# Loading the small rows ahead of tile 3's norm, and transposing the bias columns at tile 5

## The chip, the cores and the metric

The kernel runs on one core of a Trainium2 chip. A core has five engines that run side by side, each with its own in-order queue: TensorE (PE; its weight loads are listed as PEld), VectorE (DVE), ScalarE (ACT), GpSimd (POOL) and SyncE (SP), which here issues nearly all the transfers. The time is device microseconds of one execution. Lower is better.

## The reference

One layer of a hybrid decoder on 1024 tokens of width 1024, with 16 learned meta tokens in front, in float32. In outline:

```python
h = concatenate([meta, x])                         # 16 + 1024 tokens, 1024 wide
proj = rms_norm(h, norm_mix) @ w_in + b_in         # split into q, k, v, gates of two branches
log_a = log_sigmoid(g_lr @ gla_w_gate + gla_b_gate) / 16
o_gla = head_rms(gla_chunked(q, k, v, log_a)) * silu(g_r)
qk    = silu(causal_dwconv(concat[m_q, m_k], ml_conv_w, ml_conv_b))
o_ml  = head_rms(mlstm_chunked(...)) * sigmoid(m_o)
y = sigmoid(gate_a) * (o_gla @ w_branch_gla) + sigmoid(gate_b) * (o_ml @ w_branch_ml)
h = h + y @ w_out
u = causal_dwconv(rms_norm(h, norm_ffn) @ w_up, ffn_conv_w, ffn_conv_b)
h = h + (silu(gate) * up) @ w_down
out = rms_norm(h, norm_final)[16:]
```

The change touches only the start: the norm of the input tokens, and the biases that the first projections add.

## The kernel before

Matrix products are made from two-part operands: a value is split into a high part (`H`, rounded by ACT) and a low part (`L`, the rest, by DVE), and a product is the sum of three matmuls, HH, HL and LH. So `xH` and `xL` are the normalized input, channels on partitions, and `wH` and `wL` a weight.

**The input.** The tokens come in nine tiles. Tile 0 holds the 16 meta tokens, tiles 1 to 8 hold 128 tokens each; the number is that of the loop (`i`), so "the fourth tile" is tile 3 and "the sixth" is tile 5. `load_x(i)` issues the 512 KB transfer of a tile into `xt`. `norm_x(i)` then makes, for a tile: the sum of squares on ACT (L342, with a read of the accumulator), mean plus epsilon on DVE (L345), the power -1/2 on POOL (L347), scaling in place on DVE (L349; L353 for tile 1), four transposes on PE into each of two `xtp` tiles (L357), and for each of these the high part on ACT (L359) and the low part on DVE (L361). The `xtp` tiles and the tile of the column transpose share three PSUM buffers (tag `s`).

**The small rows.** `small` is a list of 21 small transfers, from a few bytes to 44 KB: ten go to `va`, which gathers biases and per-channel factors as 106 rows of 128; three to `bsm` (gate biases); two to `wg` (the decay gate's weight and bias); three to `vf` (the convolution of the FFN). (Some of the ten are listed by the trace as one row with a count.) `columns()` transposes `va` on PE into `coltp` (L323), copies it to `col` on DVE (L324) and scales four of its columns (L325). `col` holds, among others, the biases of k and q, which every eviction of their products adds.

**The first projections.** Right behind the norm come k and q of head 0, each over four spans of tokens (called thirds below, from the name of the list in the code): 0 to 272, 272 to 528, 528 to 784 and 784 to 1040 for k, and the same with a slightly shorter first span for q. Their matmuls are L159 with `wH_gk`, `wL_gk`, `wH_gq`, `wL_gq`; a span is 24 matmuls, issued in two halves of 12, k and q in turn. Each goes into one of three PSUM banks (tag `pj`), and ACT drives them out with the bias added: L446 for k (`kT`), L448 for q (`qT`). After them come the v projection (`pv`, L197) and sums and differences of the input's parts on DVE (L1033 and after), operands of a later product.

**What sets the order.** A scheduler orders the instructions of each engine by priorities and by when operands come ready by its own estimate; the written order is the base of these priorities. Evictions and the preparation of weights are given a higher priority (`hp`). Transfers are issued by SP in its own order. Each transfer counts on one of eight semaphores in turn, and waits until the one eight places earlier has landed. The raw weights (`wr`) have two buffers, so the first part of the v weights (`wr_gv`) waits until the k weights are split.

Of the kernel before, what the change touches and what calls it, by code (L numbers as in the profile page):

```python
# [25 lines left out]
NC = SEQ // P  # L26
# [19 lines left out]
def hybrid_kernel(ctx, tc, x, meta, norm_mix, w_in, b_in, gla_w_gate, gla_b_gate, gla_norm,  # L46
                  ml_conv_w, ml_conv_b, ml_norm, w_branch_gla, w_branch_ml, w_out, norm_ffn,
                  ffn_w_up, ffn_conv_w, ffn_conv_b, ffn_w_down, norm_final, out):
    nc = tc.nc
# [9 lines left out]
    def hp(n):  # L59

        return tc.high_priority(offset=max(1, min(n, tc.cur_priority - floor[0])))
# [222 lines left out]
    small = []  # L284
# [35 lines left out]
    def columns():  # L320

        tp = ps.tile([P, 512], F32, name="coltp", tag="s", bufs=3)
        nc.tensor.transpose(tp[:, :nrow], va[:nrow, :], ident[:nrow, :nrow])  # L323
        nc.vector.tensor_copy(col, tp[:, :nrow])  # L324
        nc.vector.tensor_scalar(col[:, C_GQ:C_GQ + 4], col[:, C_GQ:C_GQ + 4], QS, None, OP.mult)  # L325
# [3 lines left out]
    def load_x(*tiles):  # L329
        for i in tiles:  # L330
            n = NM if i == 0 else P
            xt = xt_tiles[i]
            nc.sync.dma_start(xt[:n, :D], meta if i == 0 else x[P * (i - 1):P * i, :])
            xts[i] = xt

    def norm_x(i):
        n = NM if i == 0 else P
        c0 = 0 if i == 0 else NM + P * (i - 1)
        xt = xts[i]
        ss = xs.tile([P, 1], F32, name=f"xss{i}", tag="ss1", bufs=3)  # L340
        junk = xs.tile([P, D], F32, name=f"xj{i}", tag="of", bufs=1)
        nc.scalar.activation(junk[:n, :D], xt[:n, :D], AF.Square, accum_out=ss[:n])  # L342
        with hp(40):
            v = xs.tile([P, 1], F32, name=f"xv{i}", tag="xv", bufs=3)
            nc.vector.tensor_scalar(v[:n], ss[:n], 1.0 / D, EPS, OP.mult, OP.add)  # L345
            rs = xs.tile([P, 1], F32, name=f"xr{i}", tag="xr", bufs=3)
            last = nc.gpsimd.tensor_tensor(rs[:n], v[:n], mhalf[:n], OP.pow)  # L347
        if i != 1:
            nc.vector.scalar_tensor_tensor(xt[:n, :D], xt[:n, :D], rs[:n], gmix[:n], OP.mult, OP.mult)  # L349
        for g in range(2):  # L350
            if i == 1:
                h = slice(512 * g, 512 * (g + 1))
                nc.vector.scalar_tensor_tensor(xt[:, h], xt[:, h], rs, gmix[:, h], OP.mult, OP.mult)  # L353
            tp = ps.tile([P, 4, P], F32, name=f"xtp{i}_{g}", tag="s", bufs=3)
            for j in range(4):
                k = 4 * g + j
                nc.tensor.transpose(tp[:, j, :n], xt[:n, k * P:(k + 1) * P], ident[:n, :n])  # L357
            h4 = xH[:, 4 * g:4 * g + 4, c0:c0 + n]
            nc.scalar.activation(h4, tp[:, :, :n], AF.Copy)  # L359
            l4 = xL[:, 4 * g:4 * g + 4, c0:c0 + n]  # L360
            nc.vector.tensor_tensor(l4, tp[:, :, :n], h4.bitcast(F32), OP.subtract)  # L361
        return last
# [11 lines left out]
    load_x(3)  # L374
    U.get(1, 0)
    load_x(4, 5)
    norm_x(3)
    U.get(2, 0)
    load_x(6, 7, 8)
    for dst, ap in small:  # L380
        nc.sync.dma_start(dst, ap)
    for i in range(4, NC + 1):
        if i == NC:
            columns()
        last = norm_x(i)
    for t, c in ((xH, 0), (xL, 32)):
# [920 lines left out]
    i = 0  # L1307
# [843 lines left out]
    i = FIRST  # L2151
# [87 lines left out]
```

## Time and profile before

| what | us |
|---|---|
| three runs | 1880.22, 1873.54, 1877.35; median 1877.35 |
| profiled execution, its own time | 1882.24 |
| its span (first to last instruction) | 1880.5 |
| PE busy in the span | 1844.2 (98%) |
| DVE, ACT, POOL busy | 1298.8, 931.1, 236.5 |
| mean granted clock of TensorE | 0.992 |

The profile is of one execution. A row of the order of time gives start, length, engine, line, operation, "out<-in" by the program's names, shapes and a count; a bracket at its end gives the idle time of the engine ahead of it and what ended that. A row of the stretches gives a stretch, its length, the busy time of PE, PEld, DVE, ACT and POOL with the number of instructions, then the clock that PE was granted (1.00 is full), the mean busy share of the transfer engines, and GB/s. A matmul's listed length is longer than the step to the next one, since they overlap.

### The profile page before, as it was taken

The page shows a single profiled execution, that of the slowest core. Times are in us where ns is not written, and L with a number is a line of the kernel's source. Part 1 is how long each engine was busy: PE and PEld are TensorE (multiplying, and loading weights), DVE is VectorE, ACT ScalarE, POOL GpSimd, SP SyncE. Part 2 cuts the span into 40 slices and gives each one's busy share as a digit, 9 for nine tenths or more (in the row PEclk, how much of TensorE's full clock was granted, in tenths as well). Part 3 has the DMA queues.
Part 4 walks back from the last instruction along what each step waited for, and adds up shares of the span by engine and source line. Part 5 has one row for each costly group of instructions (what it writes and reads, how often), then busy time and mean ns, then how long its engine had stood idle before and what let it go on. Part 6 is the DMA issues. An engine that isn't in the chain of part 4 may idle for free. (4 is left out here: it accounts for less than half of the span.)

```text
span 1880.5 us, 32830 instructions
## 1 busy us (share of the span) xinstructions
PE 1844.2 (98%) x13158; PEld 1759.1 (94%) x13158; DVE 1298.8 (69%) x1960; ACT 931.1 (50%) x1602; POOL 236.5 (13%) x220
## 2 busy tenths in 40 slices
PE   8999999999999999999999999999999999999997
PEld 6999999999999999898999999999999999987886
DVE  7755555567766467676633655888788899877877
ACT  5445444423456677876431235943443443446755
POOL 3200000000032122000000000012222222200000
PEclk9999999999999999999999999999999999999999
DMA  4244434345523233357667987433333545589985
GB/s 142 84 119 123 118 111 122 106 138 155 173 65 113 65 116 113 102 183 261 241 239 255 329 295 261 130 101 108 107 101 113 159 144 165 178 304 338 357 300 216
DMA packets 256338, 322.13 MB, mean 171 GB/s; under 512 B 14643, under 2 KB 197341, under 8 KB 254521
## 3 DMA queue, kind: packets, MB, share of 16 engines
q1 hardware_dynamic: 256089, 319.93, 51.7%
q8 instruction: 103, 1.69, 0.4%
q14 instruction: 50, 0.41, 0.1%
q0 software_dynamic: 96, 0.10, 0.0%
HBM read 231.59 MB, written 88.40 MB: 170 GB/s over the span
## 5 line engine op out<-in xcount | busy, mean ns | idle before, releaser
L1999 DVE TENSOR_TENSOR ringL<-f,ringH 128x1024 fp32r<-128x1024 f32 x76 | 80.0, 1066 | 19.9 <-ACT ringH L1998 19.5
L1998 ACT ACTIVATE ringH<-f 128x1024 fp32r<-128x1024 f32 x76 | 69.1, 928 | 36.5 <-DMA f<-in_ffn_w_down_dram 24.4
L1865 PE MATMUL po<-wH_wo,yH 128*128 128x256 f32 x256 | 73.6, 288 | 0.0
L1865 PE MATMUL po<-wL_wo,yH 128*128 128x256 f32 x256 | 73.4, 287 | 0.0
L1865 PE MATMUL po<-wH_wo,yL 128*128 128x256 f32 x256 | 73.1, 286 | 0.0
L1814 DVE SCALAR_TENSOR_TENSOR cv<-u,fc,cv 128x1024 f32<-128x1024 f32 x44 | 65.0, 1479 | 0.4
L705 POOL TENSOR_TENSOR pk<-pk,kT 128x256 f32<-128x256 f32 (+1 forms) x40 | 49.8, 1267 | 90.1 <-ACT pk L703 78.3
L1742 POOL TENSOR_TENSOR SB<-SA,rg 128x512 f32<-128x512 f32 x20 | 27.7, 1383 | 233.1 <-DVE SA L1738 120.7
L1090 POOL TENSOR_TENSOR gA<-gu2raw,gA 128x512 fp32r<-128x512 f32 x14 | 18.0, 1286 | 287.8 <-ACT gA L1089 287.8
L1724 POOL TENSOR_TENSOR A<-u2raw,A 128x512 fp32r<-128x512 f32 x20 | 42.7, 2137 | 88.4 <-ACT A L1723 88.4
L1723 ACT ACTIVATE HA<-rg 128x1024 fp32r<-128x1024 f32 x16 | 17.0, 1060 | 72.6 <-PE Y L1765 72.6
L1865 PEld LDWEIGHTS po<-wL_wo,yH 128*128 128x128 f32 x256 | 49.9, 195 | 0.0
L1865 PEld LDWEIGHTS po<-wH_wo,yL 128*128 128x128 f32 x256 | 49.8, 195 | 0.0
L1865 PEld LDWEIGHTS po<-wH_wo,yH 128*128 128x128 f32 x256 | 49.8, 194 | 0.0
L2037 ACT ACTIVATE aH<-f 128x768 fp32r<-128x768 f32 (+1 forms) x38 | 35.4, 934 | 27.9 <-PE dV L2062 14.0
L1792 ACT ACTIVATE u2raw<-X 128x258 f32<-128x258 f32 (+1 forms) x44 | 16.4, 374 | 65.6 <-PE X L1765 65.5
L2038 DVE TENSOR_TENSOR aL<-f,aH 128x768 fp32r<-128x768 f32 (+1 forms) x38 | 40.4, 1067 | 11.7 <-ACT aH L2037 11.2
L1147 ACT ACTIVATE goB<-goB,col 128x256 f32<-128x256 f32 x56 | 28.1, 502 | 37.7 <-DVE goB L1142 22.3
L1486 PE MATMUL bm<-omL,wH_bm 128*128 128x342 f32 x144 | 46.0, 320 | 0.0
L1486 PE MATMUL bm<-omH,wH_bm 128*128 128x342 f32 x144 | 46.0, 320 | 0.0
L1486 PE MATMUL bm<-omH,wL_bm 128*128 128x342 f32 x144 | 46.0, 320 | 0.0
L1147 ACT ACTIVATE goA<-goA,col 128x258 f32<-128x258 f32 (+1 forms) x56 | 28.4, 508 | 35.4 <-DVE goA L1143 28.3
(772 smaller groups left out, 7820.3 us busy)
## 6 DMA issues: line engine op xcount, KB each, us to landing
f<-wts SPq DMA_DIRECT2D x38, 512.0 KB
vr<-in_w_in_dram SPq DMA_DIRECT2D x24, 512.0 KB
wsH<-in_ffn_w_down_dram SPq DMA_DIRECT2D x11, 1024.0 KB
wts<-wsL SPq DMA_DIRECT2D x11, 1024.0 KB
rg<-in_ffn_w_up_dram SPq DMA_DIRECT2D x22, 512.0 KB
ru<-in_ffn_w_up_dram SPq DMA_DIRECT2D x22, 512.0 KB
ad<-a SPq DMA_DIRECT2D x44, 256.0 KB
wr_wo<-in_w_out_dram SPq DMA_DIRECT2D x18, 512.0 KB
```

The costliest lines, as they stand in the source:

```text
L705: nc.gpsimd.tensor_tensor(e, e, k, OP.mult)
L1090: nc.gpsimd.tensor_tensor(t[:, 4:8], g_raw, t[:, 0:4].bitcast(F32), OP.subtract)
L1147: nc.scalar.activation(v, v, func, bias=cc(c + i))
L1486: nc.tensor.matmul(pts[i][:, :n], a[:, k, :], b[k][:, t0:t0 + n], start=(k == 0 and j == 0), stop=(k == NK - 1 and j == 2))
L1724: eng.tensor_tensor(l, src, h.bitcast(F32), OP.subtract)
L1742: late.tensor_tensor(sb[:, 0:4], sa[:, 0:4], rg[:, 0:4], OP.subtract)
L1814: nc.vector.scalar_tensor_tensor(y, u[:, j:SEQ + j], fc[:, j, jj:jj + 1], y, OP.mult, OP.add)
L1865: nc.tensor.matmul(pt[:, :DV], a, b[:, k % 4, :], start=(k == 0 and i == 0), stop=(k == NK - 1 and i == len(terms) - 1))
L1998: nc.scalar.activation(h, raw, AF.Copy)
L1999: splits.append(nc.vector.tensor_tensor(l, raw, h.bitcast(F32), OP.subtract))
L2037: nc.scalar.activation(h, a[:, :n], AF.Copy)
L2038: nc.vector.tensor_tensor(l, a[:, :n], h.bitcast(F32), OP.subtract)
```

## The change

```diff
@@ -374,13 +374,13 @@
     load_x(3)
     U.get(1, 0)
     load_x(4, 5)
+    for dst, ap in small:
+        nc.sync.dma_start(dst, ap)
     norm_x(3)
     U.get(2, 0)
     load_x(6, 7, 8)
-    for dst, ap in small:
-        nc.sync.dma_start(dst, ap)
     for i in range(4, NC + 1):
-        if i == NC:
+        if i == 5:
             columns()
         last = norm_x(i)
```

The transfers of the small rows stand behind the loads of tiles 4 and 5, ahead of the first v weights and of tiles 6 to 8. The columns are transposed ahead of tile 5's norm instead of tile 8's. No instruction is added or taken away. On each engine the same instructions stand in another order, up to the end of the v projection.

On SP, behind the first tiles. Before (`xt6` is tile 6):

```order
L333 DMA xt4_96<-in_x_dram 128x1024
L333 DMA xt5_97<-in_x_dram 128x1024
L333 DMA xt6_98<-in_x_dram 128x1024
L333 DMA xt7_99<-in_x_dram 128x1024
L103 DMA wr_gv0_0_221<-in_w_in_dram 128x3x256
L103 DMA wr_gv0_0_221<-in_w_in_dram 128x3x16
L103 DMA wr_gv0_0_221<-in_w_in_dram 128x3x4
L333 DMA xt8_100<-in_x_dram 128x1024
L103 DMA wr_gv0_0_221<-in_w_in_dram 128x3x4
L381 DMA va_104<-in_b_in_dram 8x128 x4
```

With the change, from the last of the small rows on (the first of them, the same `va` row, follows `xt5`):

```order
L378 DMA vf_107<-in_ffn_conv_b_dram 44x128
L103 DMA wr_gv0_0_239<-in_w_in_dram 128x3x256
L333 DMA xt6_98<-in_x_dram 128x1024
L103 DMA wr_gv0_0_239<-in_w_in_dram 128x3x16
L103 DMA wr_gv0_0_239<-in_w_in_dram 128x3x4
L333 DMA xt7_99<-in_x_dram 128x1024
L333 DMA xt8_100<-in_x_dram 128x1024
```

Tiles 6 and 7 went from ahead of the v weights to behind them and behind all small rows.

On ACT, the squares of tiles 6 and 7 (`xj6`, `xj7`). Before:

```order
L342 ACTIVATE xj6_296,xss6_295<-xt6_98 128x1024
L342 ACTIVATE xj7_318,xss7_317<-xt7_99 128x1024
L359 ACTIVATE xH_88<-xtp3_0_207 128x4x128
L359 ACTIVATE xH_88<-xtp3_1_214 128x4x128
L359 ACTIVATE xH_88<-xtp4_0_259 128x4x128
```

And, further on, the first evictions of k and q, before:

```order
L359 ACTIVATE xH_88<-xtp6_1_310 128x4x128
L359 ACTIVATE xH_88<-xtp7_0_325 128x4x128
L359 ACTIVATE xH_88<-xtp7_1_332 128x4x128
L446 ACTIVATE kT0_385<-pj0_0_387,col_109 128x272
L446 ACTIVATE kT0_385<-pj0_272_439,col_109 128x256
L448 ACTIVATE qT0_386<-pj1_0_400,col_109 128x258
```

The same with the change, where both stand together:

```order
L359 ACTIVATE xH_88<-xtp5_0_285 128x4x128
L446 ACTIVATE kT0_385<-pj0_0_387,col_109 128x272
L359 ACTIVATE xH_88<-xtp5_1_292 128x4x128
L448 ACTIVATE qT0_386<-pj1_0_400,col_109 128x258
L342 ACTIVATE xj6_300,xss6_299<-xt6_98 128x1024
L446 ACTIVATE kT0_385<-pj0_272_439,col_109 128x256
L342 ACTIVATE xj7_322,xss7_321<-xt7_99 128x1024
L359 ACTIVATE xH_88<-xtp6_0_307 128x4x128
L359 ACTIVATE xH_88<-xtp6_1_314 128x4x128
L342 ACTIVATE xj8_344,xss8_343<-xt8_100 128x1024
```

The first evictions went from behind tile 7 to among tile 5, and the squares of tiles 6 and 7 from ahead of tile 3's high part to behind the evictions.

On DVE, around the copy of the columns, with the change:

```order
L361 TENSOR_TENSOR xL_89<-xtp4_1_266,xH_88 128x4x128
L324 COPY col_109<-coltp_273 128x106
L325 TENSOR_SCALAR col_109<-col_109 128x4
L361 TENSOR_TENSOR xL_89<-xtp5_0_285,xH_88 128x4x128
L361 TENSOR_TENSOR xL_89<-xtp5_1_292,xH_88 128x4x128
L345 TENSOR_SCALAR xv6_302<-xss6_299 128x1
L349 SCALAR_TENSOR_TENSOR xt6_98<-xt6_98,xr6_304,gmix_112 128x1024
L345 TENSOR_SCALAR xv7_324<-xss7_321 128x1
L349 SCALAR_TENSOR_TENSOR xt7_99<-xt7_99,xr7_326,gmix_112 128x1024
L361 TENSOR_TENSOR xL_89<-xtp6_0_307,xH_88 128x4x128
```

Before, the copy stood behind the low parts of tile 7; now it stands behind those of tile 4, and the scaling of tile 7 stands ahead of tile 6's low parts. On PE the second q span (`pj1_258`) went from behind tile 7's transposes to ahead of tile 6's.

## The prediction

> **What bounds the kernel now.** I read the busy times first, then PE's stretches near the start, then PE's waits and the order of time around them. One row of the page and two rows of the stretches (length; then busy time of PE, PEld, DVE, ACT and POOL; granted clock; DMA share; GB/s):
>
> ```profile
> PE 1844.2 (98%) x13158; PEld 1759.1 (94%) x13158; DVE 1298.8 (69%) x1960; ACT 931.1 (50%) x1602; POOL 236.5 (13%) x220
> ...
> 22.90:52.40 29.50, 27.32 (x215) 26.39 (x214) 26.56 (x36) 14.63 (x26) 16.23 (x30) 0.94 0.14 31
> 52.40:100.00 47.60, 47.60 (x361) 47.05 (x360) 31.97 (x47) 19.83 (x33) 5.03 (x7) 1.00 0.36 107
> ```
>
> PE sets the time. From 52.4 us on it has no idle time at all up to 100 us, so a microsecond that PE gains before 52.4 us goes on to the end unless something later takes it back. In 22.9 to 52.4 us PE is idle for 2.18 us (29.50 less 27.32) and its clock is not full. All that the change moves lies before about 88 us; behind that the order of the work on PE is the same in both kernels. So the question is what PE loses between 16 and 52 us. The order of time there (start, length, engine, line, what, and in brackets the idle time and what ended it):
>
> ```profile
> 32.21 1.17 PE L357 MATMUL xtp<-ident,xt 128*128 128x128 f32 x8 [0.27 <-DVE xt L349]
> 33.32 0.31 PE L323 MATMUL coltp<-ident,va 106*128 106x106 f32 x1
> 33.51 1.29 DVE L361 TENSOR_TENSOR xL<-xtp,xH 128x512 fp32r<-128x512 f32 x2 [0.24 <-ACT xH L359]
> 34.72 0.26 DVE L324 COPY col<-coltp 128x106 f32<-128x106 f32 x1
> 35.01 0.85 ACT L446 ACTIVATE kT<-pj,col 128x272 f32<-128x272 f32 x2 [0.99 <-DVE col L324]
> 35.55 0.39 PE L159 MATMUL pj<-xH,wH_gq 128*128 128x256 f32 x1 [1.92 <-ACT kT L446]
> ```
>
> The transpose of the bias columns (L323) is issued only at 33.32, its copy on DVE stands behind two subtractions of tile 7, the first k eviction on ACT needs that copy, and PE needs a bank of `pj`, of which there are three, all full: 1.92 us idle. It is followed by a second loss:
>
> ```profile
> 36.15:39.60 3.45, 3.45 (x19) 3.45 (x18) 2.27 (x5) 1.68 (x3) 2.92 (x10) 0.51 0.00 0
> ...
> 36.24 0.41 PE L159 MATMUL pj<-xH,wL_gq 128*128 128x256 f32 x1
> 36.67 1.91 PE L357 MATMUL xtp<-ident,xt 128*128 128x128 f32 x8
> 39.65 0.29 PE L159 MATMUL pj<-xL,wH_gq 128*128 128x256 f32 x1
> 40.95 0.28 PE L159 MATMUL pj<-xH,wH_gk 128*128 128x256 f32 x1
> 52.20 0.28 PE L159 MATMUL pj<-xH,wL_gq 128*128 128x256 f32 x1
> ```
>
> For 3.45 us the granted clock is 0.51. From 40.95 to 52.20 there are 96 matmuls, so one takes 11.25/95 = 0.118 us at full clock.
>
> **The price of the lost clock.** Between the matmuls at 36.24 and 39.65 PE issued eight matmuls and the eight transposes of tile 8. What these cost at full clock follows from tile 5:
>
> ```profile
> 27.40 0.28 PE L159 MATMUL pj<-xH,wH_gk 128*128 128x256 f32 x1
> 27.59 1.06 PE L357 MATMUL xtp<-ident,xt 128*128 128x128 f32 x8
> 28.41 0.36 PE L159 MATMUL pj<-xL,wH_gk 128*128 128x256 f32 x1
> 28.61 0.27 PE L159 MATMUL pj<-xH,wL_gk 128*128 128x256 f32 x1
> ```
>
> Two matmul steps and eight transposes took 1.21 us here, so the transposes cost 1.21 - 2 x 0.118 = 0.97 us. Eight matmuls and the transposes are 0.94 + 0.97 = 1.91 us at full clock; they took 3.41, so the half clock cost 1.50 us. Together with the waits, 1.92 + 0.27 + 1.50 = 3.69 us. That is all this change can win in the place it aims at, 0.2% of the time.
>
> **What it removes: the late column copy.** In the new order `coltp` stands among the first third's q matmuls, between the transposes of tiles 4 and 5, and its copy stands on DVE behind tile 4 instead of tile 7. The order of time around tile 4:
>
> ```profile
> 23.47 0.60 PE L357 MATMUL xtp<-ident,xt 128*128 128x128 f32 x4
> 23.49 1.29 DVE L361 TENSOR_TENSOR xL<-xtp,xH 128x512 fp32r<-128x512 f32 x2 [2.87 <-ACT xH L359]
> ```
>
> The first four transposes of tile 4 start at 23.47. From there, nine k matmuls, five q matmuls and the second half of tile 4 put `coltp` at about 26.0, its copy at 27.1 behind tile 4's last subtraction, and the first k eviction at 28.0 to 28.4. PE wants the bank for the second q third after tile 5's transposes and twelve matmuls of the second k third, at 29.5. So this wait goes, with 1.1 us to spare: minus 1.92, and with it, if no other gap comes, minus 1.50. Tile 5's scaling also goes forward, into DVE's idle 2.87 us ahead of 23.5 us, and the 0.27 us at tile 7 is replaced by what follows.
>
> **What it adds: tiles 6 and 7 are normalized late.** Before, their squares ran early; now ACT has tile 6's square behind the first q eviction, and tile 7's square behind the second k eviction (the order shown ahead). From a square to the transposes there is this chain (rows of different tiles, for their lengths and hand-overs):
>
> ```profile
> 25.43 1.05 ACT L342 ACTIVATE xj<-xt 128x1024 f32<-128x1024 f32 x1
> 26.17 1.27 DVE L349 SCALAR_TENSOR_TENSOR xt<-xt,xr,gmix 128x1024 f32<-128x1024 f32 x1
> 26.37 0.19 ACT L342 ACTIVATION_READ_ACCUMULATOR xj<-xt 128x1 f32 x1
> 28.35 0.14 DVE L345 TENSOR_SCALAR xv<-xss 128x1 f32<-128x1 f32 x1
> 28.63 0.55 POOL L347 TENSOR_TENSOR xr<-xv,mhalf 128x1 f32<-128x1 f32 x1 [3.10 <-DVE xv L345]
> ```
>
> The square and its read, 25.43 to 26.56, take 1.13 us; then 0.14 + 0.55 + 1.27 on DVE, POOL and DVE; the hand-over DVE to POOL is 0.14 (28.49 to 28.63), DVE to PE 0.15 (27.44 to 27.59), and I take 0.04 and 0.05 for the other two. Sum: 3.47 us from the start of a square to the transposes.
>
> Tile 6: its square starts behind the first q eviction, at 29.4, so its transposes can start at 32.9. PE gets there at 33.3. No stall.
>
> Tile 7: take the last matmul of the second k third as zero. Its eviction starts at 0.3 and takes 0.45, the square starts at 0.75, and the transposes of tile 7 can start at 4.2. PE in that time has eight q matmuls (1.06 with the step into them), tile 6's transposes (0.97), four q matmuls and two of the next third (0.7, and about 0.1 for restarts): it is there at 2.85. **It waits 1.37 us.** The second half of tile 7 needs a buffer of the transposes, of which there are three; it is tile 6's first one, drained by a DVE subtraction of 0.68 that stands behind tile 7's scaling: 0.25 us more. ACT's square also sits ahead of tile 6's evictions: 0.15 us. Tile 8's scaling comes behind tile 7's subtractions on DVE and is late by about 0.13 us. Together plus 1.90 us. Bounds: zero, if the squares get ahead of what I assumed; 3 us, if each hand-over is a third longer and two of the waits don't overlap.
>
> **What it moves: 21 small transfers ahead of tiles 6 to 8.** SP's rows, and the square of tile 5:
>
> ```profile
> 4.34 4.58 SPq L333 DMA_DIRECT2D xt<-in_x_dram  x4
> 15.94 1.08 ACT L342 ACTIVATE xj<-xt 128x1024 f32<-128x1024 f32 x1
> 16.73 1.44 SPq L103 DMA_DIRECT2D wr_gv<-in_w_in_dram  x3
> 18.22 0.48 SPq L333 DMA_DIRECT2D xt<-in_x_dram  x1
> 19.22 1.76 SPq L381 DMA_DIRECT2D va<-in_b_in_dram  x5
> 22.93 0.32 SPq L381 DMA_DIRECT2D va<-in_ml_conv_w_dram  x1
> 23.29 0.31 SPq L381 DMA_DIRECT2D va<-in_ml_conv_b_dram  x1
> 27.46 0.35 SPq L381 DMA_DIRECT2D vf<-in_ffn_conv_b_dram  x1
> ```
>
> SP stood still from 8.9 to 16.7 us ahead of the value weights, and the small transfers now go into that gap. They don't all fit: from the eighth on, each waits until an earlier transfer on its semaphore has landed, the eighth for tile 5, which was there by 15.94, when its square began. From the eighth's issue to the end of the last one was 4.5 us (23.29 to 27.81), so the value weights and tile 6 come at 20.4 to 21 us instead of 16.7 and 8. A 512 KB tile behind small pieces landed 4.7 us after its issue (18.22 to 22.93, where the next transfer waited for it): tile 6 by 25.7, tiles 7 and 8 by about 27.5. Their squares want them at 29.4, 33.1 and 35.4. So this costs nothing, the cover being 3.7 us for tile 6; without it each microsecond costs one. `va` is wanted at 26 and is complete by 18; `vf` is wanted at 44 and is complete by 23.
>
> **Sum.** 1882.24 (the profiled execution, span 1880.5) - 3.69 + 1.90 = 1880.45, that is 1.8 us less. The median of the three runs is 4.9 us below the profiled execution; set against it, **1875.5 us**.
>
> **The clock, the largest rival.** Whether a gap costs the clock is decided between these (two waits near 2 us and one of 1.2, and the stretch after each):
>
> ```profile
> 796.90 0.33 PE L627 MATMUL ot<-ident,or 128*128 128x128 f32 x1 [1.90 <-ACT or L615]
> 1158.30 0.65 PE L1676 MATMUL htp<-ident,hn 2*128 2x2 f32 x8 [2.22 <-ACT hn L1661]
> 759.91 0.35 PE L741 MATMUL sc<-pk 128*128 128x128 f32 x1 [1.24 <-ACT An L735]
> ...
> 796.90:800.30 3.40, 3.40 (x15) 3.01 (x15) 1.41 (x7) 2.74 (x7) 0.00 (x0) 0.57 0.54 158
> 1159.20:1162.50 3.30, 3.30 (x18) 3.30 (x17) 1.65 (x2) 2.58 (x10) 0.55 (x1) 0.50 0.96 310
> 759.90:763.30 3.40, 3.38 (x25) 3.40 (x26) 1.86 (x2) 3.33 (x9) 0.00 (x0) 1.00 0.00 0
> ```
>
> Gaps of 1.90 and 2.22 us, like the 1.92 above, were followed by some 3.4 us at half clock; a gap of 1.24 was not. The new gap, 1.37 and 0.25 with transposes between and on both sides, lies between them, nearer to the harmless one. [...]
>
> **The rivals.** B: the new gap costs the clock. Then 1.50 us comes back: -3.69 + 1.90 + 1.50 = -0.3, **1877.1**. [...] Against it: no single idle piece reaches 1.9. C: there is no gap at tile 7, since ACT reaches the square sooner than I work out; the whole 3.69 goes, **1873.7**. Against it: the square stands behind an eviction that cannot start before the k third is complete. D, the slower one: tiles 6 to 8 land late. It decides from a landing of tile 6 after 29.4 us on; if the small transfers held SP until 28 us, tile 6 would land at 32.7, PE would lose 3.3 more and the clock 1.5: -1.8 + 4.8 = +3.0, **1880.4**. For it: SP issues in order and the small transfers wait on semaphores. Against it: 3.7 us of cover. E: a later wait that PE does not lead swallows the advance, **1877.35**; such a wait would have to start from a transfer or POOL, and up to 100 us PE has none.
>
> **How the numbers follow.** The forecast (A) 0.46, B 0.28, C 0.15, D 0.06, E 0.05. All five lie within 0.3% of the median (5.6 us), about what a measurement of this kernel can tell from no change: its three runs alone lie 6.7 us apart. So faster and slower come from the scatter on top: faster 0.10, same 0.85, slower 0.05. The range takes C's and D's times with some 3 us of scatter, a little less on D's side for its chance: 1870.0 to 1880.5.
>
> **What would show it.** Right: no wait of PE on a k eviction near 33 us; `coltp` near 26 us; one wait of 1.2 to 1.6 us on tile 7's scaling (L349) between 34 and 37 us; the first `pv` matmul near 50.5 us instead of 52.4; the granted clock 1.00 in the 3.4 us after that wait (0.5 for B); SP not waiting past 21 us ahead of tile 6. Wrong: ACT waiting for a transfer ahead of tile 6's or 7's square (D), or a first `pv` matmul earlier or later than now by more than 4 us. A time outside 1870 to 1880.5 with these steps as forecast would mean that something behind 100 us moved.

## The result and the profile after

The changed kernel takes 1875.74 us (median of 22 runs, 1871.47 to 1884.02) beside 1880.01 us (22 runs, 1873.54 to 1883.87) for the kernel before: ratio 0.998, 95% interval 0.9972 to 0.9987, that is 2.4 to 5.3 us less. The time stands within 0.3 us of the forecast of 1875.5. That flatters it: the forecast started from the median of three runs, 1877.35, which more runs moved up by 2.7 us, and took 1.8 us off, where the medians show 4.3. The verdict "within 0.3%" holds.

The busy times and the two stretches of the changed kernel (columns as before: length; busy time of PE, PEld, DVE, ACT and POOL; granted clock; DMA share; GB/s):

```profile
PE 1839.3 (98%) x13158; PEld 1754.4 (94%) x13158; DVE 1299.5 (69%) x1960; ACT 930.4 (50%) x1602; POOL 246.0 (13%) x220
...
22.90:52.40 29.50, 28.20 (x238) 27.81 (x236) 22.76 (x34) 16.24 (x30) 13.09 (x25) 1.00 0.25 68
52.40:100.00 47.60, 47.47 (x362) 46.93 (x361) 35.35 (x50) 19.87 (x34) 15.22 (x14) 1.00 0.35 104
```

In the stretch that the change aims at PE is idle for 1.30 us instead of 2.18, and the clock is 1.00 instead of 0.94. What makes this up, in order of time:

```profile
25.24 0.26 PE L323 MATMUL coltp<-ident,va 106*128 106x106 f32 x1
26.43 0.26 DVE L324 COPY col<-coltp 128x106 f32<-128x106 f32 x1
27.09 0.48 ACT L446 ACTIVATE kT<-pj,col 128x272 f32<-128x272 f32 x1
31.76 0.47 ACT L446 ACTIVATE kT<-pj,col 128x256 f32<-128x256 f32 x1 [2.30 <-PE pj L159]
32.14 1.04 ACT L342 ACTIVATE xj<-xt 128x1024 f32<-128x1024 f32 x1
34.19 1.28 DVE L349 SCALAR_TENSOR_TENSOR xt<-xt,xr,gmix 128x1024 f32<-128x1024 f32 x1 [0.73 <-POOL xr L347]
35.39 0.68 DVE L361 TENSOR_TENSOR xL<-xtp,xH 128x512 fp32r<-128x512 f32 x1
35.62 1.16 PE L357 MATMUL xtp<-ident,xt 128*128 128x128 f32 x8 [1.30 <-DVE xt L349]
...
35.62:39.02 3.40, 3.40 (x29) 3.28 (x30) 3.40 (x7) 1.96 (x4) 0.55 (x1) 1.00 0.08 11
...
48.70 0.38 PE L197 MATMUL pv<-wH_gv,xH 128*128 128x280 f32 x1
```

The column transpose comes at 25.24 instead of 33.32, the first k eviction at 27.09 instead of 35.01, and PE doesn't wait for it. PE's one listed wait is the new one, on tile 7's scaling (35.62), and the 3.4 us behind it run at full clock (29 matmuls; in the first profile of the kernel before there were 19 in 3.45 us behind its wait). The first `pv` matmul comes at 48.70 instead of 52.42. SP:

```profile
7.57 2.61 SPq L378 DMA_DIRECT2D va<-in_b_in_dram  x5
11.63 0.23 SPq L378 DMA_DIRECT2D va<-in_gla_norm_dram  x1
14.13 0.27 SPq L378 DMA_DIRECT2D va<-in_ml_conv_b_dram  x1
17.58 0.35 SPq L378 DMA_DIRECT2D vf<-in_ffn_conv_b_dram  x1
18.05 0.40 SPq L103 DMA_DIRECT2D wr_gv<-in_w_in_dram  x1
18.50 0.48 SPq L333 DMA_DIRECT2D xt<-in_x_dram  x1
```

The small rows wait three times for an earlier transfer (11.63, 12.91 and 14.13), the value weights follow at 18.05 and tile 6 at 18.50. No square of tiles 6 to 8 waits for a transfer.

### The profile page after: what moved, and what is told of

It is laid out like the page before. It is cut to its first block, busy times and chain, and to the rows that moved or that the text cites. A ratio compares the mean times of both kernels' runs of the same rounds, so it can differ in the third digit from the quotient of the medians.

```text
span 1874.4 us, 32829 instructions
## 1 busy us (share of the span) xinstructions
PE 1839.3 (98%) x13158; PEld 1754.4 (94%) x13158; DVE 1299.5 (69%) x1960; ACT 930.4 (50%) x1602; POOL 246.0 (13%) x220
## 5 line engine op out<-in xcount | busy, mean ns | idle before, releaser
L1147 ACT ACTIVATE goA<-goA,col 128x258 f32<-128x258 f32 (+1 forms) x56 | 28.4, 508 | 35.7 <-DVE goA L1143 28.3
```

The costliest lines, as they stand in the source:

```text
L1147: nc.scalar.activation(v, v, func, bias=cc(c + i))
```

## The experiments

The theory on trial, called the theory of the place below: the whole difference arises between tile 3's transposes and the first `pv` matmul (the wait on the column copy and its half clock go, the gap at tile 7 comes), and goes on to the end one for one. Its rivals: that the gain comes from the transfers; that a later wait swallows part of it; and, for the clock, that the new gap costs it. For each kernel the length from the start of tile 3's transposes to the start of the first `pv` matmul was read from the order of time:

| profile of | tile 3 | first pv | between | PE's listed waits between | clock behind |
|---|---|---|---|---|---|
| before, first | 21.88 | 52.42 | 30.54 | 0.27 + 1.92 | half |
| before_again | 20.38 | 48.96 | 28.58 | 0.27 + 1.91 | full |
| before_third | 20.25 | 48.81 | 28.56 | 0.25 + 1.91 | full |
| before_fourth | 21.31 | 51.50 | 30.19 | 0.26 + 1.92 | half |
| changed, first | 21.39 | 48.70 | 27.31 | 1.30 | full |
| after_again | 21.28 | 48.48 | 27.20 | 1.30 | full |
| after_third | 21.19 | 48.39 | 27.20 | 1.30 | full |
| small_only | 21.09 | 53.45 | 32.36 | 0.35 + 1.00 + 0.39 + 2.65 | half |
| cols_only | 21.33 | 47.68 | 26.35 | none | full |
| cols_again | 21.59 | 47.98 | 26.39 | none | full |
| x67_first | 21.11 | 47.48 | 26.37 | 0.29 | full |
| x67_again | 20.87 | 47.25 | 26.38 | 0.29 | full |
| gap_half | 21.09 | 51.58 | 30.49 | 0.54 + 1.30 + 0.83 | half |
| gap_full | 22.01 | 49.36 | 27.35 | 0.22 + 0.46 + 0.41 | full |

In the last column half is a granted clock of 0.50 to 0.54 in the 3.4 us behind PE's last listed wait. Full is 1.00 there in before_again, before_third and the three profiles of the changed kernel, and 1.00 over the whole stretch from 22.90 to 52.40 us in cols_only, cols_again and x67_again. In x67_first and gap_full eight transposes behind a wait took 1.06 and 1.07 us, beside 1.91 at a clock of 0.51 in the first profile of the kernel before.

### Half of the change: the rows early, the columns late

```diff
-        if i == 5:
+        if i == NC:
             columns()
```

> Only half of the change: the small rows are loaded ahead of tile 3's norm, the columns are transposed ahead of tile 8's norm as before. Theory of the place (the whole gain is PE's wait on the column copy, 1.92 us, and the half clock behind it, 1.50 us, less the new gap at tile 7, 1.30 us): the column copy is late again, so PE waits on the first k eviction again for at least 1.9 us; since the squares of tiles 6 and 7 stand late on ACT here (behind tile 5's high parts), the copy may be up to 2 us later than before, so that wait is 1.9 to 4 us, with up to 1 us more at tile 6. Time 0 to 3 us above the kernel before, ratio 1.000 to 1.0015. Theory of the transfers (the gain comes from the small rows leaving SP's queue early, which brings something forward from the start on): the gain stays without the columns, 3 to 4 us below the kernel before, ratio about 0.998.

Measured: 1881.98 us (11 runs) beside 1879.77, ratio 1.001, interval 0.9998 to 1.0022. PE's waits, and the stretch behind the last:

```profile
32.08 1.17 PE L357 MATMUL xtp<-ident,xt 128*128 128x128 f32 x8 [1.00 <-DVE xt L349]
33.64 0.31 PE L323 MATMUL coltp<-ident,va 106*128 106x106 f32 x1 [0.39 <-DVE xL L361]
36.61 0.38 PE L159 MATMUL pj<-xH,wH_gq 128*128 128x256 f32 x1 [2.65 <-ACT kT L446]
...
36.61:40.01 3.40, 3.40 (x17) 3.40 (x18) 2.07 (x4) 1.42 (x4) 2.33 (x7) 0.54 0.21 32
```

The wait on the k eviction is back, longer by 0.73 us, since the late squares push the copy back, and the stretch behind it is at half clock. The early transfers alone win nothing: that rival falls, and the time is where the theory of the place put it.

### The other half: the columns early, the rows late

```diff
     load_x(4, 5)
-    for dst, ap in small:
-        nc.sync.dma_start(dst, ap)
     norm_x(3)
     U.get(2, 0)
     load_x(6, 7, 8)
+    for dst, ap in small:
+        nc.sync.dma_start(dst, ap)
     for i in range(4, NC + 1):
         if i == 5:
             columns()
```

> The other half: the loads as before (tiles 6 and 7 early, small rows behind tile 8), the columns transposed ahead of tile 5's norm. Before, the last of the column rows was issued at about 23.9 us, so they are there by about 26; the transpose stands at about 26 to 27 on PE. Theory of the place: no wait on a k eviction, no half clock at 36 us, and no gap at tile 7 either, since the squares of tiles 6 and 7 stay early on ACT; PE may wait up to 0.5 us for the column rows. Time 3.2 to 3.7 us below the kernel before, ratio 0.998, and 0.5 to 1.5 us below the changed kernel. Theory of the transfers: nothing is won, ratio 1.000. If the column rows land later than I read it, PE stands at the transpose in order, and each microsecond of that costs one.

Measured: 1879.24 us (11 runs) beside 1879.77, ratio 0.9995, interval 0.9983 to 1.0006. The time missed the forecast, but the place did what it should:

```profile
24.06 0.30 SPq L381 DMA_DIRECT2D va<-in_norm_ffn_dram  x1
28.96 0.26 PE L323 MATMUL coltp<-ident,va 106*128 106x106 f32 x1
29.89 0.26 DVE L324 COPY col<-coltp 128x106 f32<-128x106 f32 x1
30.18 0.49 ACT L446 ACTIVATE kT<-pj,col 128x272 f32<-128x272 f32 x1 [3.72 <-DVE col L324]
...
22.90:52.40 29.50, 29.36 (x244) 28.55 (x243) 29.06 (x41) 16.36 (x28) 18.09 (x36) 1.00 0.21 49
```

The last column row is issued at 24.06, the transpose comes at 28.96, and the first k eviction at 30.18 is still in time for PE: the stretch has 29.36 us of PE in 29.50. So either something behind took the gain back, or the eleven runs were drawn badly. The same kernel again:

> The early columns with the old loads once more. In the first eleven runs it was 0.5 us below the kernel before (by medians), where its profile has the first pv matmul 4.7 us earlier. If the place decides, and the first eleven runs were drawn badly (slow starts: tile 2 landing late, PE at half clock at 16 us), the ratio is 0.998 to 0.9985 now. If a later wait takes the gain back in this order of loads, it is 0.9995 again, and the profile shows the same late waits as the first one (2.6 us at the htp transposes near 1208 us, 2.5 us at dY near 1657 us).

Measured: 1874.69 us (11 runs) beside 1879.72, ratio 0.9979, interval 0.9968 to 0.999. Its profile has the same late waits, of 2.63 us at 1206.72 and 2.55 at 1654.51, so their length doesn't decide. (Behind the first of them the clock was 0.52 for 3.4 us in the first profile, where it was 2.64 us long, and 1.00 in this one.) The means of the two sets of runs differ by 3.4 us, with 2.1 either way, which is more than the scatter inside each set makes likely. They ran on two chips, on which the kernel before took the same (1879.77 and 1879.72). So that the first eleven runs were a poor draw is the likeliest reading, but it isn't shown. The 22 runs together lie 2.3 us below all runs of the kernel before, with 1.3 either way (means, 95%). Here the old loads suffice: this profile needs the early columns, and not the early rows, to be rid of the wait.

### Tiles 6 and 7 ahead of the rows

```diff
-    load_x(4, 5)
+    load_x(4, 5, 6, 7)
     for dst, ap in small:
         nc.sync.dma_start(dst, ap)
     norm_x(3)
     U.get(2, 0)
-    load_x(6, 7, 8)
+    load_x(8)
```

> The changed kernel with tiles 6 and 7 loaded ahead of the small rows. Their squares then stand early on ACT, as before the change, and the columns stay early. Theory of the place: the gap of 1.30 us at tile 7's scaling goes and nothing takes its place: 1.3 us below the changed kernel, 3.4 to 3.7 below the kernel before, ratio 0.998. Rival: the square of tile 8 and the split of the value weights now stand ahead of the second k eviction on ACT, and PE waits for its bank up to 1.5 us: no better than the changed kernel.

Measured: 1874.82 us (11 runs) beside 1879.77, ratio 0.998, interval 0.9971 to 0.999. The gap at tile 7's scaling is gone, and what is left stands at tile 8's:

```profile
25.35 0.26 PE L323 MATMUL coltp<-ident,va 106*128 106x106 f32 x1
26.55 0.49 ACT L446 ACTIVATE kT<-pj,col 128x272 f32<-128x272 f32 x1 [2.12 <-DVE col L324]
36.41 1.06 PE L357 MATMUL xtp<-ident,xt 128*128 128x128 f32 x8 [0.29 <-DVE xt L349]
```

The second k eviction comes late on ACT, as the rival had it (34.75 instead of 31.76), but PE doesn't wait for it.

> Tiles 6 and 7 ahead of the small rows, and early columns, a second time, as the version that may beat both. From tile 3's transposes to the first pv matmul 26.4 us, 0.9 less than the changed kernel; ratio to the kernel before 0.998 to 0.9985, below the kernel before by 3 to 4 us. Against the changed kernel a difference of 0.9 us stays below what these runs can tell.

Measured: 1876.38 us (12 runs) beside 1879.89, ratio 0.9978, interval 0.9967 to 0.999. The place repeats to 0.01 us (26.38). All 23 runs lie 3.9 us (0.9 either way) below the kernel before, the 34 runs of the changed kernel 3.4 (1.0 either way). So the 0.9 us that the profiles show between the two can't be told from nothing by time.

### The same kernels again

> The changed kernel once more, beside the others. Theory of the place: ratio 0.9972 to 0.9987 to the kernel before; one gap of 1.2 to 1.4 us at tile 7's scaling, clock 1.00 behind it. The first matmul of the projections at 15.5 us in the first profile of the changed kernel and at 16.0 in that of the kernel before: if that half microsecond is scatter of tile 2's landing, it moves by some tenths here; if it belongs to the change, it is 15.5 again.

Measured: 1877.37 us (11 runs) beside 1879.77, ratio 0.9986, interval 0.9976 to 0.9997. The gap is 1.30 us again, with the clock at 1.00 behind it. The first projection matmul came at 16.40 instead of 15.47: the half microsecond at the start was scatter (tile 2's square began at 7.62 us here and at 6.01 in the first profile).

> The kernel before as one of the tried ones: its ratio to itself shows what this measurement tells from no change (1.000, interval about 0.999 to 1.001), and its profile is a second one to compare with. The wait on the k eviction near 35.5 us should be there with 1.9 us, and the stretch at half clock behind it; the start may be early (first projection matmul at 15.2 to 15.5 us, full clock) or late (16.0 to 16.5, half clock), whichever way tile 2 lands.

Measured: 1879.94 us (11 runs) beside 1879.72 of the same kernel, ratio 1.0005, interval 0.9992 to 1.0019. The wait, and the 3.4 us behind it, in this profile and in before_fourth:

```profile
33.70 0.39 PE L159 MATMUL pj<-xH,wH_gq 128*128 128x256 f32 x1 [1.91 <-ACT kT L446]
...
33.70:37.10 3.40, 3.40 (x29) 3.40 (x30) 3.03 (x5) 1.89 (x4) 2.32 (x7) 1.00 0.01 2
```

```profile
34.63 0.58 PE L159 MATMUL pj<-xH,wH_gq 128*128 128x256 f32 x1 [1.92 <-ACT kT L446]
...
34.63:38.03 3.40, 3.40 (x16) 3.40 (x17) 1.84 (x4) 1.39 (x3) 2.33 (x7) 0.50 0.00 0
```

Here is the step that the prediction took for certain and that is not: the same wait of the same kernel is followed by 29 matmuls at full clock in one execution, and by 16 at half clock in another.

> The kernel before once more, for its profile alone. In the first profile the wait of 1.92 us on the k eviction was followed by 3.4 us at half clock, in the second (1.91 us) by none. If the half clock belongs to the wait, it is there now; if it comes or goes by execution, as behind the equal waits of 1.9 us near 509, 797 and 1158 us, either. From tile 3's transposes to the first pv matmul: 30.5 us with it, 28.6 without.

Measured, in one run each: before_third took 1878.39 us, with the wait at 1.91, no half clock, and 28.56 us between tile 3 and `pv`.

> As before_third: 30.5 us from tile 3's transposes to the first pv matmul with the half clock, 28.6 without; nothing between is expected.

Measured: 1878.49 us, half clock, 30.19 us. Two of the four profiles of the kernel before have it. It costs 30.19 - (28.58 + 28.56)/2 = 1.6 us when it comes. The first profile's 30.54 holds 0.33 us more that isn't the wait's: PE's slow start reaches into tile 3 there, and from tile 3's transposes to tile 4's it is 1.59 us (21.88 to 23.47), beside 1.26 in before_fourth (21.31 to 22.57).

> The changed kernel once more, for its profile alone: a gap of 1.30 us at tile 7's scaling and the clock at 1.00 behind it, 27.2 to 27.3 us from tile 3's transposes to the first pv matmul, as in its two profiles so far. If the clock falls behind this gap too in some executions, it is 28.7 and the prediction's rival B is a part of the truth.

Measured: 1874.50 us in one run, gap 1.30, clock 1.00, 27.20 us. The three profiles of the changed kernel agree within 0.11 us.

### The gap at tile 7 made longer

```diff
-        nc.scalar.activation(junk[:n, :D], xt[:n, :D], AF.Square, accum_out=ss[:n])
+        for w in (512, D) if i == 7 else (D,): nc.scalar.activation(junk[:n, :w], xt[:n, :w], AF.Square, accum_out=ss[:n])
```

(512 columns and then all of them in gap_half, all of them twice in gap_full.)

> The changed kernel with one more ACT operation: a square over half of tile 7 ahead of tile 7's own square (its result is overwritten), so that PE's gap at tile 7's scaling grows from 1.30 us to 1.8 to 2.0. It is the cost of the largest rival of the prediction (the new gap costs the clock), put on trial. If the length of the gap decides (in the profiles so far every gap of PE up to 1.43 us kept the clock, and of those from 1.58 us on nearly all lost it for about 3.4 us): the gap is followed by a granted clock of 0.5 to 0.7, 1.5 us are lost on top of 0.6, the first pv matmul comes at 50.7 (48.6 in the changed kernel) and the time is 1 to 1.5 us below the kernel before, ratio 0.9993. If the transposes around it decide, nothing new: the clock stays, pv at 49.2, ratio 0.9985.

Measured: 1877.91 us (11 runs) beside 1879.72, ratio 0.9991, interval 0.9983 to 1.0. The gap didn't grow in one piece:

```profile
34.16 0.39 PE L159 MATMUL pj<-xH,wH_gk 128*128 128x256 f32 x1 [0.54 <-ACT xH L359]
35.96 0.63 PE L357 MATMUL xtp<-ident,xt 128*128 128x128 f32 x4 [1.30 <-DVE xt L349]
37.41 0.93 PE L357 MATMUL xtp<-ident,xt 128*128 128x128 f32 x4 [0.83 <-DVE xv L345]
...
37.41:40.81 3.40, 3.40 (x17) 3.40 (x18) 3.00 (x5) 0.78 (x2) 0.55 (x1) 0.53 0.45 87
```

With the longer square the scheduler also put the split of the value weights between tile 6's evictions. PE gets there later and waits in pieces: 0.54, 1.30, and, behind four transposes, 0.83. Behind that the clock is 0.53 for 3.4 us. The waits are 1.37 us longer than the changed kernel's, and the stretch to `pv` is 3.2 us longer; that the clock makes the other 1.9 is inferred from the difference. Behind 30 us no wait of 1.30 us alone or of 0.8 alone cost the clock in any profile (66 cases of 0.8 to 1.35 us, all at 0.99 or more behind); here, where the two came together, it was 0.53. That is rival B's price. How the waits add up is read in the rivals below and in the last section.

> The same with the whole square of tile 7 done twice, the second behind tile 6's evictions: the gap grows to about 3.4 us. If a microsecond of this gap costs one microsecond of the whole, and a gap above 1.6 us the clock: pv at 52 to 52.5 as in the kernel before, and the time of the kernel before, ratio 0.999 to 1.001. If a later wait swallows such differences (the rival by which an advance at the start is not worth its size at the end), the time stays at the changed kernel's, ratio 0.998.

Measured: 1877.89 us (12 runs) beside 1879.72, ratio 0.999, interval 0.9981 to 1.0. Its premise failed:

```profile
35.06 0.39 PE L159 MATMUL pj<-xL,wH_gk 128*128 128x256 f32 x1 [0.22 <-DVE xL L361]
38.14 1.07 PE L357 MATMUL xtp<-ident,xt 128*128 128x128 f32 x8 [0.46 <-DVE xt L349]
41.16 0.63 PE L357 MATMUL xtp<-ident,xt 128*128 128x128 f32 x4 [0.41 <-DVE xt L349]
```

The scheduler put tile 7's transposes behind more matmuls here, so no wait is over half a microsecond and the stretch is as long as the changed kernel's (27.35). It therefore doesn't tell whether a wait of 3.4 us would be swallowed later.

### Place and time together

Against the mean of the four profiles of the kernel before (29.47 us between tile 3 and `pv`), and against all of its 118 runs (mean 1879.84 us), with the 95% interval from the scatter of the runs:

| kernel | by the place | by the time | runs |
|---|---|---|---|
| changed | -2.2 | -3.4 ± 1.0 | 34 |
| cols_only | -3.1 | -2.3 ± 1.3 | 22 |
| x67_first | -3.1 | -3.9 ± 0.9 | 23 |
| small_only | +2.9 | +2.2 ± 1.7 | 11 |
| gap_half | +1.0 | -1.6 ± 1.0 | 11 |
| gap_full | -2.1 | -1.8 ± 1.2 | 12 |

Four of the six agree within their interval; the changed kernel is just outside, and gap_half by 1.6 us. For gap_half there is one profile, and it has the half clock; without the 1.9 us put down to it the place would give -0.9. For the changed kernel some 1.2 us stay that its place doesn't account for. Whether they are scatter of the four profiles of the kernel before (two with the half clock, two without) or lie behind 52 us isn't settled. No later wait that would hold them was found.

## Why the prediction was right or wrong

**What bounds the kernel, and where the change acts: right.** PE is 98% busy; the difference arises between 22.9 and 52.4 us, and from 52.4 to 100 us PE is idle for 0.13 us after the change.

**The wait on the column copy goes: right, with its times forecast about a microsecond late.** `coltp` was forecast at about 26.0 and came at 25.24, the first k eviction at 28.0 to 28.4 and came at 27.09. No wait on a k eviction is left in any kernel with early columns.

**The half clock, 1.50 us: taken for certain, and it is not.** The step "minus 1.92, and with it, if no other gap comes, minus 1.50" read one execution. The wait is followed by the half clock in two of four profiles, at 1.6 us a time. So the size of the term was right, and its certainty wrong: it is worth 0.8 us on the mean of the four, and 0 or 1.6 in a single execution. Which of the two it is goes, in the four profiles, with where the wait falls in the windows of the last section: with 1.92 and 1.99 us of idle in one window the clock fell, with 1.30 and 0.88 or 1.06 and 1.11 in two it stayed. In the sum for the profiled execution it belonged; carried over to the median of the runs, as the prediction did, only its mean did.

**The new gap: the main piece right, the three small pieces wrong.** Forecast 1.37 us at tile 7's scaling; measured 1.30 in all three profiles. The further 0.25 (the buffer of tile 6's first transposes), 0.15 (tile 6's evictions behind the square) and 0.13 (tile 8) didn't come. The subtraction that frees the buffer stands behind tile 7's scaling as said, but it ends at 36.07 (35.39 + 0.68), and the second half of tile 7 wants the buffer some 0.5 us after 35.62, at 36.1. I had let PE want it at once. Tile 6's transposes at 32.51 and tile 8's at 40.41 have no listed wait. So the new waits are 1.30 instead of 1.90.

**The sum.** For before_fourth, with the half clock, the waits and the clock give -(1.92 + 0.26 + 1.6) + 1.30 = -2.5 us, and the stretch shortened by 30.19 - 27.24 = 3.0 (27.24 is the mean of the changed kernel's three); without the half clock it is -2.18 + 1.30 = -0.9 and 28.57 - 27.24 = 1.3. The rest, 0.4 to 0.5 us, is in no listed wait. That it lies in the order of the matmuls is likely and not shown. With the mean of the clock's cost the terms give -2.18 - 0.8 + 1.30 = -1.7, the forecast's number to 0.1, but by two errors that cancel: 0.6 us too much of new waits, and 0.7 too much of lost clock. So the agreement is luck. With the rest it is -2.1. The time shows more: -2.4 to -5.3 in the 22 runs, -3.4 ± 1.0 in all 34. The first `pv` matmul, forecast near 50.5, came 1.8 us earlier, at 48.70: 0.6 us are the small waits that didn't come, 0.5 an earlier tile 3 (21.39 instead of 21.88), 0.2 a slow start that reaches less far into it (1.36 us to tile 4 instead of 1.59), 0.1 the clock's price (1.6 instead of 1.50), and 0.4 the rest.

**The transfers: harmless, as forecast, though the time was late.** The value weights were forecast at 20.4 to 21 us and went out at 18.05, tile 6 at 18.50. The eighth small transfer (`conv_b`) went out at 14.13, where I had it wait for tile 5 until 15.94, and from it to the end of the last one were 3.8 us (17.58 + 0.35 - 14.13) instead of 4.5. So rival D was further off than its chance of 0.06 says.

**The rivals.** B, the new gap costs the clock: not in three profiles; its price is real, as gap_half shows, where two waits add up. Transposes alone didn't bring it: in small_only PE did nothing but sixteen transposes from 30.07 to 33.48 us, with 1.2 us idle, and the clock was 1.00 in that stretch and in the next:

```profile
30.07:33.48 3.41, 2.18 (x16) 1.61 (x16) 2.53 (x4) 2.80 (x5) 0.90 (x2) 1.00 0.01 2
33.48:36.90 3.42, 0.60 (x3) 0.43 (x4) 3.38 (x6) 1.92 (x5) 0.20 (x1) 1.00 0.32 76
```

In gap_half the idle time alone is enough to explain the loss: from 34.23 to 37.65 us the two waits make 2.13 us, and 1.88 to 3.02 us in a window were followed by half clock in 27 cases of 28 (the last section). In after_again the 1.30 us lie whole in one window (33.69 to 37.11), and the clock stays at 1.00. C, no gap: only in cols_only and nearly in x67_first, by keeping the squares early. E, swallowed later: small_only, cols_only and x67_first show their place at the end within their intervals, so nothing large is.

**The chances.** The time fell into "same" with 0.85. The whole interval is below 1, and its lower end, 0.9972, stops just short of the 0.3%, to which I had given 0.10.

## What to carry to other kernels

One profile of a kernel is one draw. A loss that depends on the clock has to be read from several executions before it is put into a sum, and a sum made on the profiled execution must not be set against the median as it stands. When an operand is needed early, look for the smallest move that makes it early: here the columns alone did it (cols_only), or with the two tiles ahead of the small rows (x67_first), and neither has the new gap that the change bought with the late squares. Above all, a long wait can be dearer than its length (the 1.92 us here cost 1.6 us more in two of four profiles), and two short ones within 3.4 us can add up to a long one (1.30 and 0.83 us in gap_half's one profile, with the clock at 0.53 behind them).

## What the runs showed of the hardware

**In these profiles the loss of the clock behind a wait goes with PE's idle time in windows of 3.41 us.** In the 14 profiles, single waits of PE behind 30 us and the granted clock in the 3.4 us behind them:

| wait, us | cases | clock under 0.9 behind | clock 0.99 or more |
|---|---|---|---|
| 0.8 to 1.35 | 66, the two pieces of gap_half aside | 0 | 66 |
| 1.4 to 1.7 | 10 | 5 | 4 |
| 1.7 to 1.95 | 30 | 19 | 8 |
| 2.0 to 3.3 | 19 | 15 | 4 |

(The cases that are left out lie between 0.9 and 0.99.) Length alone doesn't decide. Behind a wait of 2.63 us, in cols_again, the clock was 1.00 for 3.4 us, and behind the wait of 1.92 us it was 0.51 and 0.50 in two executions of four:

```profile
1206.72 1.09 PE L1676 MATMUL htp<-ident,hn 128*128 128x128 f32 x8 [2.63 <-ACT hn L1661]
```

Nor can the five losses of the second row be laid to the waits alone. All stand at L658, whose matmuls use 17 of the 128 partitions, and behind the same narrow matmuls at 631 to 637 us the clock falls in eight of the 14 profiles without any wait. The window of these matmuls in the first profile of the kernel before, and the stretch behind it:

```profile
633.57:636.98 3.41, 3.41 (x14) 2.09 (x14) 0.87 (x1) 3.25 (x11) 1.45 (x2) 1.00 0.68 201
637.00:640.40 3.40, 3.40 (x11) 2.81 (x10) 0.00 (x0) 3.35 (x5) 0.00 (x0) 0.50 0.36 108
```

What it goes with stands in the traces' records of the clock. In each profile the granted clock changes only at times that lie whole multiples of 3.4133 us apart, to 1 ns, from the first change to the last (in before_fourth the first of them stand at 20.95, 34.60 and 38.02 us, four windows and one apart); where this grid stands differs from execution to execution. Here are windows of the grid around the wait of the kernel before, in its first profile and then in before_again, and around the wait of 2.63 us in cols_again:

```profile
32.82:36.24 3.42, 1.50 (x11) 1.15 (x11) 3.18 (x7) 1.98 (x4) 0.00 (x0) 1.00 0.02 3
36.24:39.65 3.41, 3.41 (x18) 3.41 (x17) 2.23 (x3) 1.68 (x3) 2.97 (x10) 0.50 0.00 0
```

```profile
29.42:32.83 3.41, 2.11 (x15) 1.46 (x14) 3.17 (x5) 1.53 (x3) 0.00 (x0) 1.00 0.53 73
32.83:36.25 3.42, 2.54 (x22) 2.55 (x23) 3.05 (x6) 2.31 (x5) 1.60 (x4) 1.00 0.01 2
```

```profile
1202.43:1205.84 3.41, 1.66 (x14) 1.45 (x12) 3.41 (x8) 1.38 (x2) 2.82 (x2) 1.00 0.87 284
1205.84:1209.25 3.41, 2.53 (x22) 2.53 (x23) 1.53 (x3) 3.41 (x8) 0.64 (x1) 1.00 0.02 7
```

In the first profile the whole wait lies in one window, PE is idle for 1.92 us of it (3.42 - 1.50), and the next window is at 0.50. In before_again an edge of the grid cuts the wait: 1.30 and 0.88 us are idle in the two windows, and the clock is 1.00 behind both. The other two profiles agree: 1.99 us idle in one window and the clock lost in before_fourth, 1.06 and 1.11 us and the clock kept in before_third. In cols_again the cut leaves 1.75 and 0.88 us; in cols_only a wait of 2.64 us at the same place left 2.46 us in one window, and the clock fell (0.52 in the 3.4 us behind the wait). Counted over all windows behind 30 us at full clock, those with the narrow matmuls aside:

| PE idle in the window, us | windows | next window at half clock |
|---|---|---|
| 0.50 to 1.39 | 146 | 0 |
| 1.40 to 1.87 | 18 | 5 |
| 1.88 to 3.02 | 28 | 27 |

So 1.88 to 3.02 us of idle in a window were enough in 27 of 28 cases, and 0.50 to 1.39 us in none of 146. What decides between 1.40 and 1.87 us isn't shown here.

**The clock column can miss a slow start.** The first matmuls of the kernel before, in two of its profiles (before_again first, then the first profile):

```profile
17.80 0.43 PE L159 MATMUL pj<-xL,wH_gk 128*128 128x272 f32 x1
18.03 0.43 PE L159 MATMUL pj<-xH,wL_gk 128*128 128x272 f32 x1
...
16.90:18.90 2.00, 2.00 (x10) 2.00 (x10) 2.00 (x5) 1.97 (x3) 1.06 (x1) 0.50 0.78 195
```

```profile
19.29 0.43 PE L159 MATMUL pj<-xH,wL_gk 128*128 128x272 f32 x1
19.51 0.42 PE L159 MATMUL pj<-xL,wH_gq 128*128 128x258 f32 x1
...
16.90:21.60 4.70, 4.70 (x21) 4.70 (x22) 3.72 (x6) 2.79 (x8) 2.59 (x3) 1.00 0.81 195
```

A step of 0.22 to 0.23 us stands beside a clock of 0.50 in the one and of 1.00 in the other, where full speed is 0.12 from one matmul to the next (0.118 from 40.95 to 52.20 us of the first profile, at 256 columns). The records of the clock begin only at 22.58 us in the first profile, so the column has nothing to show ahead of that. PE is at full speed from about 19.2 us on in before_again and from about 22.6 in the first profile. So PE's start is slow in both executions, for a time that differs between them, and the number of matmuls in a stretch tells it better than the clock's column. Together with the start of the first matmul (15.39 to 16.01) it moves tile 3 by 1.6 us between profiles of one kernel (20.25 to 21.88), most of what the whole change wins behind it (2.2).
